# The first stage of a hybrid attention and RWKV block: modulation weights summed in whole rows, x normed in place, one-pass transposes kept in SBUF, and 128 rows in the decay's lower terms

## The chip, the cores and the metric

The kernel runs on one core of one Trainium2 chip. The metric is the device time of one execution in microseconds (us). Before the change it is 1717.37 us, the median of three runs (1715.96 to 1721.29).

## What is computed

The block takes x (1024 tokens by 1024 columns) and a conditioning vector c, everything in float32. The part that matters here is its beginning:

```python
mod = silu(c) @ w_mod + b_mod                  # w_mod is 1024 x 6144
shift1, scale1, gate1, shift2, scale2, gate2 = split(mod, 6)
u = rms_norm(x, ln1_g) * (1 + scale1) + shift1
proj = u @ w_in                                # q k v f | r k v xw xa xg | gates
p = p + (token_shift(p) - p) * mu              # on the RWKV part
w_log = -softplus(-(w0 + tanh(xw) @ w2)) - 0.5
a = sigmoid(a0 + xa @ a2)
g = sigmoid(xg) @ g2
# ... then attention, the RWKV recurrence, their merge, and a convolutional feed-forward layer
```

Only shift1 and scale1 are needed before the first projection. The columns xw and xa (64 each) and xg (128) of the projection are its "low" columns, two tiles of 128 output channels; they come first, since the decay and the gates of the recurrence are made from them.

## The kernel before, in words

All products are made channel by channel: a tile of 128 weight columns is TensorE's stationary operand, and 512 tokens (one "half" of the sequence) are streamed through. For float32 accuracy each operand is split into an upper part (rounded to fp32r) and a lower part (the rest), and a product is the sum of three: upper x upper, lower x upper and upper x lower. So u is held as u_hi and u_lo, eight tiles of 128 channels by 1024 tokens each, and each weight tile as hi and lo. The order of TensorE (PE) is the order of the code in the whole kernel. In the first stage, the prelude, the same holds for VectorE (DVE), ScalarE (ACT) and SyncE (SP, which issues the DMAs); behind it a scheduler orders those.

The prelude goes over 16 blocks: eight channel tiles `kt`, two halves each. Its steps in the code before:

- `load_x` (L408) loads x in eight row tiles, `square` (L415) makes the sums of squares on ACT, and `norm_x` (L419) makes 1/rms (`rstd`) and writes it into diagonal matrices `dg` of 128x128.
- `mod_load` (L426) loads, for one channel tile, the 128 columns of shift1 and of scale1 from all 1024 rows of w_mod, in runs of 128 values (512 bytes). `mod_scale` (L439) sums the scale on PE in eight one-column products; `mod_shift` (L443) sums the shift on DVE in eight steps of 128x128, and `mod_sum` (L453) adds over the partitions on PE. `mod_col` (L456) adds the bias and makes A1 = (1 + scale1) * ln1_g.
- `turn` (L461) multiplies four x tiles by the diagonals, which transposes and norms them in one product; `u_upper` (L467) applies A1 and the shift on ACT and casts to u_hi; `u_lower` (L473) makes u_lo on DVE.
- `low_part` (L477) makes the six products of a block with the two low weight tiles (24 and 25 of w_in). They are summed over the eight channel tiles in four PSUM banks.
- `warm` (L434) issues products without use, which only keep PE busy.
- At the end `low_out` (L490) shifts the sums by one token, and `w2l` (L567, on POOL, the GpSimd engine) is made: the lower part of w2 and a2. Its rows 0 to 63 hold w2's, its rows 64 to 127 a2's. w2 and a2 stand twice one above the other in `w2h`.

Then `shifted` (L346) makes k, r and v of the first head pair (`ps_rkv`: 24 products of 512 columns each, from weight tiles 16, 12 and 20), and between these products `lora` (L603) makes the decay and a, in eight groups of four products `zp`: for each of w2 and a2, w2h with the 128 rows of `xs` (64 rows of its upper part, 64 of its lower), then `w2l` with the 64 rows of the upper part alone (L628). PSUM for `ps_rkv` has two banks, so the third (v) waits for the evacuation of the first (k), which is an instruction of DVE, L358. A ring of two buffers, `raw`, holds every weight tile on its way in (L249, L486), and w2 too.

Of the kernel before, what the change touches and what calls it, by code (L numbers as in the profile page):

```python
# [15 lines left out]
D = 1024  # L16
S = 1024
KT = 8
# [113 lines left out]
def hybrid_block(ctx: ExitStack, tc: tile.TileContext, a, out):  # L132
# [13 lines left out]
    def f32(ap):  # L146
        return ap.bitcast(F32)
# [187 lines left out]
    with ExitStack() as es:  # L335
# [63 lines left out]
        w2l = xp.tile([128, 512], F32R, name="w2l")  # L399
# [3 lines left out]
        with tc.tile_pool(name="st", bufs=1) as st, tc.tile_pool(name="stp", bufs=2, space=PS) as stp, \  # L403
                tc.manual_schedule(engines={mybir.EngineType.SP, mybir.EngineType.DVE, mybir.EngineType.Activation}):
            ssq = st.tile([128, 8], F32, name="ssq")
            rstd = st.tile([128, 8], F32, name="rstd")

            def load_x(half):  # L408
                xs = []
                for t in range(half * 4, half * 4 + 4):  # L410
                    xs.append(st.tile([128, D], F32, tag="xt", name=f"xt{t}", bufs=8))
                    nc.sync.dma_start(xs[-1], a["x"][t * 128 : t * 128 + 128, :])
                return xs

            def square(t):  # L415

                nc.scalar.activation(u_lo[:, 6 + t // 4, :], xs[t], AF.Square, accum_out=ssq[:, t : t + 1])

            def norm_x(half):  # L419

                hs = slice(half * 4, half * 4 + 4)
                rms_rstd(rstd[:, hs], ssq[:, hs])
                for j in range(half * 4, half * 4 + 4):
                    ts(dg[:, j, :], ident, rstd[:, j : j + 1], None, op0=ALU.mult)

            def mod_load(kt):  # L426

                ws = [st.tile([128, D], F32, tag="mw", name=f"wm{i}{kt}", bufs=9) for i in range(2)]
                for i, w in enumerate(ws):
                    nc.sync.dma_start(w.rearrange("p (c n) -> p c n", n=128),  # L430
                                      a["w_mod"].rearrange("(c p) n -> p c n", p=128)[:, :, i * D + kt * 128 : i * D + kt * 128 + 128])
                return ws

            def warm(n):  # L434

                for _ in range(n):
                    mm(idle[:, 0:NC1], cst[:, 0:128], cst, start=True, stop=True)

            def mod_scale(kt, ps):  # L439
                for ci in range(KT):  # L440
                    mm(ps[:, 1:2], mw[kt][1][:, ci * 128 : ci * 128 + 128], sc[:, ci : ci + 1], start=ci == 0, stop=ci == KT - 1)

            def mod_shift(kt):  # L443
                acc = st.tile([128, 128], F32, tag="acc", name=f"acc{kt}", bufs=2)
                for ci in range(KT):
# [1536 lines left out]
```

## Time and profile before

| | |
|---|---|
| time, median of three runs | 1717.37 us (1715.96 to 1721.29) |
| profiled execution, from its first to its last instruction (span) | 1713.2 us; the median of the runs lies 4.2 us above it |
| PE busy in the span | 1665.3 us (97%) |
| DVE, ACT, POOL busy | 1213.0, 813.1, 143.5 us |
| mean granted TensorE clock | 0.986 |
| prelude: first product of `ps_rkv` | 88.04 us after the span's start |
| granted clock, 60 to 70 us | 0.50 |

How to read the profile: a row of the timeline has the start in us, the length in us, the engine, the line of the code, the operation, what it writes and reads, its shape and how many equal ones follow each other; in brackets stands how long the engine sat idle before it and what ended that. PEld is PE's weight load, which overlaps its products. A row of the table by stretches has, for each engine, busy us and the number of instructions, then the clock granted to TensorE (1.00 is full), the DMA engines' share and GB/s.

### The profile page before, as it was taken

The numbers are of one execution on the slowest core, as the hardware profiler recorded it, in microseconds if no ns is written. First come the engines' busy times: TensorE is split into PE (matmuls) and PEld (weight loads), VectorE is DVE, ScalarE is ACT, GpSimd is POOL, SyncE is SP. The second block draws the span as 40 slices with busy tenths as digits, with TensorE's granted clock in tenths as the row PEclk, the third lists the DMA queues.
The fourth block names the chain that finished last, engine by engine and source line by source line (L and its number), as shares of the span: only waits on it lengthen the run. The fifth ranks groups of instructions, "written<-read, shape, count | busy, mean of one in ns | idle before, by whom it ended". The sixth has DMA issues, their size and how long they took to land.

```text
span 1713.2 us, 26506 instructions
## 1 busy us (share of the span) xinstructions
PE 1665.3 (97%) x9984; PEld 1367.0 (80%) x9984; DVE 1213.0 (71%) x2432; ACT 813.1 (47%) x1482; POOL 143.5 (8%) x175
## 2 busy tenths in 40 slices
PE   8899999999999999999999999999999999999998
PEld 7867777787777777888878888888888888888886
DVE  4576687777677632889777734897777777786677
ACT  5364343334344454766652314664444444454455
POOL 0001011111110002323212100000000000000000
PEclk9899999999999999999999999999999999999999
DMA  9287644533333226434268611132333223484463
GB/s 310 89 304 236 185 133 112 140 96 116 95 96 98 85 81 158 135 100 125 75 231 288 255 50 62 57 105 98 106 116 111 93 99 117 149 293 153 123 215 111
DMA packets 135311, 239.87 MB, mean 140 GB/s; under 512 B 39888, under 2 KB 64720, under 8 KB 135184
## 3 DMA queue, kind: packets, MB, share of 16 engines
q1 hardware_dynamic: 127232, 220.94, 39.8%
q0 software_dynamic: 7952, 17.25, 3.7%
q8 instruction: 78, 1.28, 0.3%
q14 instruction: 49, 0.40, 0.1%
HBM read 172.59 MB, written 65.54 MB: 139 GB/s over the span
## 4 chain that ended last, share of the span: by engine, by line
PE 80%; DVE 9%; DMA 4%; ACT 3%; SPq 2%; issue 1%; DVEq 0%; ACTq 0%; POOLq 0%
PE X L140 13%; PE D L140 12%; PE Y L140 6%; PE wo L140 5%; PE gt L140 5%; PE br L140 5%; PE ps_rkv L140 5%; PE qk L140 4%; PE rk_ps L140 4%; PE W L140 3%; PE lg L140 2%; PE ov L140 2%; PE tr L140 2%; PE sp L140 2%; PE tp L144 2%
## 5 line engine op out<-in xcount | busy, mean ns | idle before, releaser
L140 PE MATMUL D<-op,op 128*128 128x512 f32 x924 | 209.8, 389 | 0.0
L140 PEld LDWEIGHTS D<-op,op 128*128 128x128 f32 x924 | 173.3, 188 | 36.3 <-DVE op L1245 0.3
L140 PE MATMUL X<-T_m,S 128*128 128x512 f32 x440 | 107.3, 390 | 0.1
L140 PEld LDWEIGHTS X<-T_m,S 128*128 128x128 f32 x440 | 82.4, 188 | 18.2 <-ACT T_m L1670 0.6
L1244 ACT CAST op<-g 128x512 fp32r<-128x512 f32 x77 | 47.8, 621 | 73.0 <-PE D L140 47.9
L1245 DVE TENSOR_TENSOR op<-g,op 128x512 fp32r<-128x512 f32 x77 | 53.0, 689 | 40.9 <-ACT op L1244 40.8
L1481 DVE SCALAR_TENSOR_TENSOR c<-ab,vec,c 128x512 f32<-128x512 f32 x88 | 65.9, 749 | 19.5 <-ACT c L1484 17.9
L263 DVE TENSOR_TENSOR lo_in<-raw_in,hi_in 128x512 fp32r<-128x512 f32 x84 | 56.4, 706 | 31.6 <-PE gt L140 12.3
L796 DVE TENSOR_TENSOR t<-E,M 128x60 f32<-128x60 f32 (+24 forms) x248 | 56.8, 229 | 29.5 <-DMA M<-sm 24.2
L1445 DVE TENSOR_TENSOR S<-ur,S 128x512 fp32r<-128x512 f32 x66 | 45.5, 691 | 35.6 <-ACT S L1441 35.5
L261 ACT CAST hi_in<-raw_in 128x1024 fp32r<-128x1024 f32 x42 | 43.9, 1047 | 52.5 <-PE ps_rkv L140 17.2
L1441 ACT CAST S<-ur 128x512 fp32r<-128x512 f32 x66 | 41.0, 622 | 55.6 <-DVE ur L1434 30.6
L1445 DVE TENSOR_TENSOR A<-ur,A 128x512 fp32r<-128x512 f32 x64 | 44.0, 688 | 30.9 <-ACT A L1441 30.7
L140 PE MATMUL Y<-T_h,A 128*128 128x512 f32 x264 | 63.5, 389 | 0.0
L140 PE MATMUL Y<-T_h,S 128*128 128x512 f32 x264 | 63.3, 389 | 0.0
L140 PE MATMUL X<-B_b,A 128*128 128x512 f32 x252 | 60.8, 390 | 0.0
L140 PE MATMUL W<-B_f,A 128*128 128x512 f32 x252 | 60.6, 389 | 0.0
L1066 ACT ACTIVATE P<-lg,nm 128x896 f32<-128x896 f32 (+3 forms) x64 | 47.5, 744 | 22.1 <-DVE nm L1062 21.9
L140 PEld LDWEIGHTS Y<-T_h,A 128*128 128x128 f32 x264 | 49.6, 188 | 10.4
L798 DVE TENSOR_TENSOR E<-E,t 128x60 f32<-128x60 f32 (+24 forms) x248 | 53.7, 216 | 5.8
L140 PEld LDWEIGHTS Y<-T_h,S 128*128 128x128 f32 x264 | 49.5, 188 | 10.3
L1441 ACT CAST A<-ur 128x512 fp32r<-128x512 f32 x64 | 39.9, 623 | 34.2 <-PE X L140 31.5
(472 smaller groups left out, 4213.3 us busy)
## 6 DMA issues: line engine op xcount, KB each, us to landing
raw_in<-in_w_in SPq DMA_DIRECT2D x50, 512.0 KB, 3.7
wm<-in_w_mod SPq DMA_DIRECT2D x48, 512.0 KB, 6.5
ur<-in_w_up SPq DMA_DIRECT2D x44, 512.0 KB, 4.0
g<-d_g SPq DMA_DIRECT2D x35, 512.0 KB, 3.9
d_g<-gs SPq DMA_DIRECT2D x44, 256.0 KB, 2.0
d_g<-c SPq DMA_DIRECT2D x33, 256.0 KB, 4.4
d_st<-qh SPq DMA_DIRECT2D x64, 128.0 KB, 2.4
d_gate<-gs SPq DMA_DIRECT2D x32, 256.0 KB, 2.6
```

Source lines behind the costliest of these rows:

```text
L140: nc.tensor.matmul(o, lhsT, rhs, start=start, stop=stop, skip_group_check=more)
L144: nc.tensor.transpose(o, i, eye)
L261: nc.scalar.copy(hi, raw)
L263: nc.vector.tensor_tensor(lo[:, c : c + NH], raw[:, c : c + NH], f32(hi[:, c : c + NH]), op=ALU.subtract)
L796: tt(tv, E32[:, 0:J, s : s + 1].to_broadcast([128, J, W]), M32[:, s : s + 1, s + 1 : 32].to_broadcast([128, J, W]), op=ALU.mult)
L798: tt(E32[:, 0:J, s + 1 : 32], E32[:, 0:J, s + 1 : 32], tv, op=ALU.add)
L1066: nc.scalar.activation(e[:, 0:n], lg[:, 0:n], AF.Exp, bias=nm[:, 0:1], accum_out=nm[:, 1:2])
L1244: nc.scalar.copy(hi, src)
L1245: tt(lo, src, f32(hi), op=ALU.subtract)
L1441: nc.scalar.copy(hi, src)
L1445: tt(lo, src, f32(hi), op=ALU.subtract)
L1481: stt(c, ab[:, x + hf * NH : x + hf * NH + NH], V("conv_w", 22 * x + i), c, op0=ALU.mult, op1=ALU.add)
```

## The change

1. w_mod is loaded in 16 whole pieces (rows ci x 128 to ci x 128 + 127 of one of the two segments, 1024 columns in one run of 4 KB). DVE alone sums them, eight into acc0 (shift) and eight into acc1 (scale), in steps of 128x1024; PE adds over the partitions in eight one-column products per segment. The pieces go through a ring of seven buffers: three of their own (`mw`) and four that held x tiles 0 to 3 (`xa`), so piece 3 is loaded when the first half of x has been transposed. Load m+7 takes the buffer of piece m.
2. x is scaled by rstd in place, on DVE, in steps of 128x1024; `turn` transposes it as it is, with the identity and in one pass, and ACT copies the result to `xn`, which keeps all of it. The transposes thus no longer wait for the modulation.
3. When both sums are there, `u_full` applies A1 and the shift on DVE, in place in `xn`, and ACT casts to u_hi. The 16 blocks follow in one run: first weight tile 24 alone for blocks 0 to 2, tile 25 behind its split from block 3 on.
4. `warm` issues 16 products at the start (before: 34, 10 and 16) and four of 512 columns on w_mod pieces later. The table of the sigmoid is loaded before the blocks.
5. `w2l` is made for all 128 rows, and `lora` multiplies it with all 128 rows of `xs`, which adds the product of the two lower parts.

The core of the diff:

```diff
-        w2l = xp.tile([128, 512], F32R, name="w2l")
+        w2l = xp.tile([128, S], F32R, name="w2l")
...
+            def ring(tag, name, dt=F32):
+                return st.tile([128, D], dt, tag=tag, name=name, bufs=3 if tag == "mw" else 4)
+            def mod_load(seg, ci):
+                w = pieces[seg, ci] = ring("mw" if len(pieces) % 7 < 3 else "xa", f"wm{seg}{ci}")
+                nc.sync.dma_start(w, a["w_mod"][ci * 128 : ci * 128 + 128, seg * D : seg * D + D])
...
+                for t in range(half * 4, half * 4 + 4):
+                    ts(xs[t], xs[t], rstd[:, t : t + 1], None, op0=ALU.mult)
             def turn(kt, half):
                 ps = stp.tile([128, NH], F32, tag="tp", name=f"tr{half}_{kt}")
                 for j in range(4):
-                    mm(ps[:, j * 128 : j * 128 + 128], xs[half * 4 + j][:, kt * 128 : kt * 128 + 128], dg[:, half * 4 + j, :], start=True, stop=True)
+                    transpose(ps[:, j * 128 : j * 128 + 128], xs[half * 4 + j][:, kt * 128 : kt * 128 + 128], ident)
+                nc.scalar.copy(xn[:, kt, half * NH : half * NH + NH], ps)
+            def mod_add(seg, ci, cols=slice(0, D)):
+                w, s_ = pieces[seg, ci][:, cols], sc[:, ci : ci + 1]
+                if ci == 0:
+                    ts(acc[seg][:, cols], w, s_, None, op0=ALU.mult)
+                else:
+                    stt(acc[seg][:, cols], w, s_, acc[seg][:, cols], op0=ALU.mult, op1=ALU.add)
...
+            def u_full(n):
+                kt, _, cs = block(n)
+                ts(xn[:, kt, cs], xn[:, kt, cs], A1[:, kt : kt + 1], m1[:, kt : kt + 1], op0=ALU.mult, op1=ALU.add)
+                nc.scalar.copy(u_hi[:, kt, cs], xn[:, kt, cs])
...
+            for t in range(4):
+                square(t)
+            norm_x(0)
+            for m in range(3):
+                mod_add(*order[m])
+            for kt in range(KT):
+                turn(kt, 0)
+            for m in range(3, 10):
+                mod_load(*order[m])
+            for t in range(4, 8):
+                square(t)
+            for m in (3, 4):
+                add_ahead(m)
+            norm_x(1)
+            for kt in range(KT):
+                turn(kt, 1)
+            nc.scalar.preload_act_table_set("sigmoid_and_others")
+            for m in range(5, 15):
+                add_ahead(m)
+                if m == 7:
+                    shift_ps = mod_sum(0, 0, KT)
+                if m == 9:
+                    mod_col(0, 0, KT, shift_ps)
+                if m > 10:
+                    warm(1, pieces[order[m]])
+            low.append(low_load(25))
+            low_split(0)
+            for x in range(2):
+                mod_add(1, KT - 1, halves_[x])
+            scale_ps = [mod_sum(1, x * 4, 4) for x in range(2)]
+            mod_col(1, 0, 4, scale_ps[0])
+            u_full(0)
+            mod_col(1, 4, 4, scale_ps[1])
+            for n in range(16):
+                if n < 15:
+                    u_full(n + 1)
+                u_lower(n)
+                low_part(0, n)
+                if n == 2:
+                    low_split(1)
+                if n == 3:
+                    for m in range(3):
+                        low_part(1, m)
+                if n > 2:
+                    low_part(1, n)
+            nc.scalar.copy(w2h, w2)
...
-                nc.gpsimd.tensor_tensor(w2l[rs, :], w2[rs, js], f32(w2h[rs, js]), op=ALU.subtract)
+                nc.gpsimd.tensor_tensor(w2l[:, js], w2[:, js], f32(w2h[:, js]), op=ALU.subtract)
...
-                    yield from lora(p, [(j, [(w2h[:, j * 512 : j * 512 + 512], xs2[j]), (w2l[HS[j]], xs2[j][HS[j]])], None, b) for j, b in enumerate(("w0", "a0"))])
+                    yield from lora(p, [(j, [(w2h[:, j * 512 : j * 512 + 512], xs2[j]), (w2l[:, j * 512 : j * 512 + 512], xs2[j])], None, b) for j, b in enumerate(("w0", "a0"))])
```

Behind the prelude PE's order is the same in both, row for row. Three places in the order are spoken of in the prediction. The first is PE at the end of the first channel tile. Before, the sums of the modulation (`mod`), the transposes (`tr0_1`: half 0, tile 1) and the products of a block (`low`) take turns:

```order
L140 MATMUL mod1_312<-cst_73,acc1_321 128x1
L140 MATMUL tr0_1_337<-xwa_124,xt0_140 128x128
L140 MATMUL tr0_1_337<-xwa_124,xt1_142 128x128
L140 MATMUL tr0_1_337<-xwa_124,xt2_144 128x128
L140 MATMUL tr0_1_337<-xwa_124,xt3_146 128x128
L140 MATMUL low01_225<-u_hi_110,hi_in24_154 128x512
L140 MATMUL low11_227<-u_hi_110,hi_in25_158 128x512
```

Now all 64 transposes stand ahead of the first sum, and both sums and the four `idle` products (with pieces 11 to 14 of w_mod, `wm13` to `wm16`) ahead of the first product of a block:

```order
L144 MATMUL tr1_7_314<-cst_73,xt7_163 128x128
L140 MATMUL mod00_334<-cst_73,acc0_139 128x1 x8
L140 MATMUL idle_142<-wm13_263,cst_73 128x512
L140 MATMUL idle_142<-wm14_321,cst_73 128x512
L140 MATMUL idle_142<-wm15_324,cst_73 128x512
L140 MATMUL idle_142<-wm16_331,cst_73 128x512
L140 MATMUL mod10_369<-cst_73,acc1_140 128x1 x4
L140 MATMUL mod14_374<-cst_73,acc1_140 128x1 x4
L140 MATMUL low00_361<-u_hi_110,hi_in24_329 128x512
L140 MATMUL low00_361<-u_hi_110,lo_in24_330 128x512
```

The transposes were between the products of the blocks and are now ahead of them, and a sum for all eight channel tiles stands where a sum for one stood.

The second place is DVE while w_mod is summed. Before, one channel tile's sum took two rows, of 128x128, between two blocks:

```order
L448 TENSOR_SCALAR acc1_321<-wm01_168,sc_90 128x128
L450 SCALAR_TENSOR_TENSOR acc1_321<-wm01_168,sc_90,acc1_321 128x128 x7
L457 TENSOR_TENSOR m1_103<-mod1_312,vec_72 128x2
L459 SCALAR_TENSOR_TENSOR A1_102<-m1_103,vec_72 128x1
L475 TENSOR_TENSOR u_lo_111<-uf1_0_309,u_hi_110 128x512
```

Now it is a run of 128x1024 steps, with one that reads PE's sum of the shift (`mod00`, row L460) among the scale's; the names count segment and piece, so `wm12` is piece 2 of the scale:

```order
L450 SCALAR_TENSOR_TENSOR acc0_139<-wm07_250,sc_90,acc0_139 128x1024
L448 TENSOR_SCALAR acc1_140<-wm10_252,sc_90 128x1024
L450 SCALAR_TENSOR_TENSOR acc1_140<-wm11_254,sc_90,acc1_140 128x1024
L460 TENSOR_TENSOR m1_103<-mod00_334,vec_72 128x8
L450 SCALAR_TENSOR_TENSOR acc1_140<-wm12_260,sc_90,acc1_140 128x1024
```

Row L460 is new in this place: the scale's last six additions stand behind it on DVE, and its own input behind all transposes on PE.

The third place is DVE some way behind the prelude, where k of the first head pair (`k00`) is evacuated. Before:

```order
L221 SCALAR_TENSOR_TENSOR acc2_866<-wm2_1_883,sc_90,acc2_866 128x1024
L648 TENSOR_TENSOR wf_1034<-wr_1035,wf_1034 128x8x8
L358 SCALAR_TENSOR_TENSOR k00_746<-ps_rkv40_766,omu_80,sh_rkv40_791 128x512
L352 MEMSET sh_rkv00_829 128x1
L584 TENSOR_TENSOR xs0_739<-xwa_124,xs0_739 64x1024
```

Now, in the changed kernel's line numbers (13 higher from L567 on):

```order
L221 SCALAR_TENSOR_TENSOR acc2_702<-wm2_1_719,sc_90,acc2_702 128x1024
L661 TENSOR_TENSOR wf_870<-wr_871,wf_870 128x8x8
L597 TENSOR_TENSOR xs0_575<-xwa_124,xs0_575 64x1024
L358 SCALAR_TENSOR_TENSOR k00_582<-ps_rkv40_602,omu_80,sh_rkv40_627 128x512
L352 MEMSET sh_rkv00_665 128x1
```

The lower part of `xs0` (64x1024) has moved from behind the evacuation of k to ahead of it.

177 lines of the change are left out of this document (66 added, 111 removed).

## The prediction

> **What bounds the kernel now.** I read the first part of the page, then the chain of work that ended last, then the table by stretches, then the timeline of the first 130 us.
>
> ```profile
> PE 1665.3 (97%) x9984; PEld 1367.0 (80%) x9984; DVE 1213.0 (71%) x2432; ACT 813.1 (47%) x1482; POOL 143.5 (8%) x175
> ...
> PE 80%; DVE 9%; DMA 4%; ACT 3%; SPq 2%; issue 1%; DVEq 0%; ACTq 0%; POOLq 0%
> ```
>
> PE sets the end: it is busy for 97% of the span, and 80% of the chain is its own. Behind the prelude its order does not change, so what the prelude saves arrives at the end, unless PE then waits for something that was early before. The question is when the first product of `ps_rkv` starts, which I call E. The table by stretches (columns as in the section on the profile) shows where the prelude loses time:
>
> ```profile
> 50.00:60.00 10.00, 5.86 (x34) 5.12 (x34) 4.21 (x11) 3.64 (x5) 0.00 (x0) 0.84 0.44 144
> 60.00:70.00 10.00, 10.00 (x40) 9.14 (x40) 4.28 (x13) 1.40 (x2) 0.00 (x0) 0.50 0.10 37
> ```
>
> PE stands idle for four of the ten us from 50, and in the next ten it is "busy" with 40 products at half clock. The timeline tells why:
>
> ```profile
> 49.23 9.36 SPq L249 DMA_DIRECT2D raw_in<-in_w_in  x2
> ...
> 55.81 1.04 ACT L261 CAST hi_in<-raw_in 128x1024 fp32r<-128x1024 f32 x1 [6.84 <-DMA raw_in<-in_w_in]
> ...
> 60.96 3.41 PE L140 MATMUL mod<-sc,wm 128*128 128x1 f32 x16
> ...
> 88.04 1.99 PE L140 MATMUL ps_rkv<-u_hi,hi_in 128*128 128x512 f32 x8
> ...
> 91.68 1.98 PE L140 MATMUL ps_rkv<-u_hi,lo_in 128*128 128x512 f32 x8
> ```
>
> The cast of a later weight stands in ACT's queue ahead of the next u_hi and waits for its load, ACT 6.84 us with it; PE runs dry and its clock falls. E is 88.04. The sixteen products from there to 91.68 take 3.64 us, 0.228 each at full clock.
>
> **The change, part by part.** First, how fast the pieces of w_mod come:
>
> ```profile
> 14.00:20.00 6.00, 5.96 (x34) 5.87 (x33) 2.74 (x7) 3.36 (x5) 0.00 (x0) 0.72 1.02 404
> 22.00:42.00 20.00, 19.23 (x118) 17.50 (x119) 10.50 (x32) 9.68 (x18) 0.00 (x0) 0.91 1.20 291
> ```
>
> From 14 to 20 us mostly whole rows (x, w_in) were in flight, at 404 GB/s; from 22 to 42 mostly w_mod in runs of 512 bytes, at 291 with busier DMA engines. A piece of 512 KB takes 1.30 us at the one rate and 1.80 at the other; I take 1.30 for whole rows. The Trainium skill (DMA: Bandwidth & Descriptors, Specifications) asks only for 512 bytes per transfer to reach the full rate, so by it the pieces would come no faster than before; the two rows speak against it, and in the sum below 1.80 would move E by 1 us at most, since DVE adds the pieces later than they land.
>
> Now PE's clock. In the first 30 us the trace has a stretch like the new prelude, with transposes and one-column products alone:
>
> ```profile
> 26.57 1.84 PE L140 MATMUL mod<-sc,wm 128*128 128x1 f32 x16
> ```
>
> ```profile
> 28.00:30.00 2.00, 1.35 (x10) 1.26 (x10) 1.42 (x6) 0.20 (x1) 0.00 (x0) 0.87 1.23 294
> 30.00:32.00 2.00, 2.00 (x9) 1.81 (x9) 0.44 (x1) 0.74 (x1) 0.00 (x0) 0.50 1.19 294
> ```
>
> Behind it the clock is at 0.50, though PE's row says busy. The new order puts all 64 transposes and the sums in one such run, so I take half clock from the 16 idle products at the start to the first `low` product, and full clock as the other end. The Trainium skill (TensorE: Matmul & The Clock Gate, Part 4) says that transposes do not count as work for the clock, which is the same choice; were they to count, the second rival below would hold.
>
> The other prices:
>
> ```profile
> 11.36 0.21 ACT L288 ACTIVATE rstd<-rstd 128x4 f32<-128x4 f32 x1
> ...
> 21.11 1.06 ACT L417 ACTIVATE u_lo<-xt 128x1024 fp32r<-128x1024 f32 x1
> ...
> 22.30 1.06 ACT L417 ACTIVATE u_lo<-xt 128x1024 fp32r<-128x1024 f32 x1
> ...
> 85.87 0.62 ACT L471 CAST u_hi<-uf 128x512 fp32r<-128x512 f32 x1
> ...
> 86.52 0.69 DVE L475 TENSOR_TENSOR u_lo<-uf,u_hi 128x512 fp32r<-128x512 f32 x1 [1.60 <-ACT u_hi L471]
> ...
> 93.56 0.75 DVE L219 TENSOR_SCALAR acc<-wm,sc 128x1024 f32<-128x1024 f32 x1
> ...
> 104.47 2.61 DVE L221 SCALAR_TENSOR_TENSOR acc<-wm,sc,acc 128x1024 f32<-128x1024 f32 x2
> ...
> 191.74 0.27 PE L144 MATMUL vt<-cst,v 128*128 128x128 f32 x1
> 191.85 0.27 PE L144 MATMUL at<-cst,ar 128*128 128x128 f32 x1
> ```
>
> ```profile
> L1521 ACT COPY x<-X 128x512 f32<-128x512 f32 x22 | 12.9, 586 | 26.3 <-PE X L140 26.3
> ```
>
> ```profile
> L507 DVE TENSOR_TENSOR lo_in<-raw_in,hi_in 128x1024 fp32r<-128x1024 f32 x2 | 2.4, 1224 | 2.7 <-ACT hi_in L505 2.7
> L1072 DVE TENSOR_SCALAR P<-P,nm 128x512 f32<-128x512 f32 x8 | 3.9, 487 | 0.3
> ```
>
> ```profile
> raw_in<-in_w_in SPq DMA_DIRECT2D x8, 512.0 KB, 4.0
> ```
>
> With these the new prelude runs as follows, the loads of the first four x tiles being unchanged.
>
> - rstd is there at 11.57, and four scalings of 0.75 end at 14.6. A tile's four one-pass transposes take 4 x 0.11 at full clock, 0.88 at half, 0.9 with the handover; ACT's copy (0.59) hides behind that. Eight tiles: 21.8 (22 with the last copy).
> - Tile 7's first transpose, at 20.9, frees the first x buffer for piece 3; it lands 4.0 later, at 25, the others 1.30 apart, and piece 15, the last of 13 transfers behind it, at 41.9. Piece 3 and 4 are added (1.31 each) by 27.6. ACT squares the other x tiles behind its copies, 4 x 1.19 + 0.5, until 27.3. Four scalings: 30.6.
> - Second half of the transposes: 37.9. Behind them on PE stands the sum of the shift, 16 one-column passes, 3.41 at half clock: 41.3. DVE has three additions and two of the scale's done by 36.6 and then stands at row L460, which waits for that sum; the last six additions are queued behind it. This is the new wait of the change: 4.7 us (1.6 if the clock is full).
> - From 41.5: 0.2, five additions 6.5, the split of weight 24 1.22, two half additions of 0.7 each: 50.1 for the first, 50.8.
> - Four sums on PE, 1.7 at half clock: 51.9. Two small steps (0.4), u_full (0.49), the cast (0.62): the first `low` product at 53.5. The second four sums and their steps let DVE finish u_full(1) at 54.5 and u_lower(0) at 55.2.
> - Then a block costs DVE 0.49 + 0.69 = 1.18: u_lower(2) at 57.5. The cast of weight 25 ends on ACT at 58.5, its split on DVE at 59.8, u_lower(3) at 61.0. Block 3's last product of weight 24 waits for that, and 84 products follow it: 84 x 0.228 = 19.2. DVE's own rest is 12 x 1.18 + 1.3 for one weight = 15.5, so PE is last. E is 80.2, against 88.04: **-7.8**. If the clock is full throughout, transposes take 5.6 per half, the sums half, and the same sum gives 74.0: -14.0.
>
> Second, the lower terms of the decay. One of the eight groups:
>
> ```profile
> 107.75 0.39 PE L140 MATMUL zp<-xs,w2h 128*128 128x512 f32 x1
> ...
> 108.07 0.50 PE L140 MATMUL zp<-xs,w2l 64*128 64x512 f32 x1
> ...
> 108.50 0.49 PE L140 MATMUL zp<-xs,w2h 128*128 128x512 f32 x1
> ...
> 108.92 0.49 PE L140 MATMUL zp<-xs,w2l 64*128 64x512 f32 x1
> ...
> 109.34 0.50 PE L140 MATMUL ps_rkv<-u_hi,lo_in 128*128 128x512 f32 x1
> ```
>
> Four products take 1.59; the step from 128 to 64 rows and back costs each of them about 0.2. With 128 rows throughout they are like all others, 4 x 0.228 = 0.91. Eight groups: 8 x 0.68 = **-5.4** on PE, which is the path here. The other end is nothing, if ACT or DVE cannot follow; I take the whole, since PE has no gap there, and DVE and ACT are busy for little more than half of the time:
>
> ```profile
> 110.00:120.00 10.00, 10.00 (x34) 5.48 (x32) 5.19 (x7) 5.89 (x9) 0.49 (x1) 1.00 1.01 386
> ```
>
> Third, what comes late behind E:
>
> ```profile
> 82.50 0.33 SPq L249 DMA_DIRECT2D raw_in<-in_w_in  x1
> ...
> 98.03 0.74 DVE L358 SCALAR_TENSOR_TENSOR k<-ps_rkv,omu,sh_rkv 128x512 f32<-128x512 f32 x1
> ...
> 98.83 1.22 DVE L584 TENSOR_TENSOR xs<-xwa,xs 64x1024 fp32r<-64x1024 f32 x1
> 98.93 2.10 PE L140 MATMUL ps_rkv<-u_hi,hi_in 128*128 128x512 f32 x8
> ```
>
> The 48 products of k and r end about when k is evacuated, and v's first product at 98.93 waits for that evacuation. Now the lower part of `xs0` (1.22) stands ahead of it on DVE, which has no gap there: **+1.2**, between 0 and 1.2. Behind it zp and the next evacuations wait, and they have time. The load of weight 20 waits for w2l, made before when 5.5 us of the prelude were left (82.50). Now w2h is cast after the last u_hi (about 76), w2l by 80, and the load lands at E + 4; SP holds the loads of segment 2 behind it, and DVE's first addition of those, before at E + 5.5, would see at worst 2 us more. I take 0, since they land at E + 5.
>
> At no cost: fewer idle products (before, they filled waits), the sigmoid's table load (ACT waits for the weight there) and w2l's further rows on POOL (the length of a row is the same).
>
> Sum: -7.8 - 5.4 + 1.2 = -12.0 on a span of 1713.2, 1701.2, and with the 4.2 us between span and median 1705.4. I predict 1705.
>
> **The rivals.** *The clock stays full* (transposes count, or the four idle products hold it): -14.0 - 5.4 + 1.2 = -18.2, 1699. For it: in the stretch from 26 to 30 PE also waited, and the new run of transposes is denser. Against it: the row at 30 to 32.
>
> *The lower terms save nothing* (the change does not do what it says there): DVE or ACT sets the pace from E + 14 to E + 37, and 1705.4 + 5.4 = 1711. DVE is then behind with the sums of segment 2; but the profile has no PE idle there now.
>
> *The old wait comes back*: the cast of weight 16 stands on ACT ahead of u_hi(7), and its load is issued only when weight 25 is split, at 59.8. With 4.0 us it lands just as ACT arrives; with 6.6, as at 49.23, PE still has blocks 4 to 6 to do. If it took 10, PE would lose 3.7 us, and if the clock then fell for 13.6 us, as around 60 to 70, half of that as well: about 10 us, 1716, no change.
>
> *Slower*: half clock through all products of the blocks, as before from 60 to 70. 84 x 0.456 = 38.3 instead of 19.2, E at 99.3: +11.3 + 1.2 - 5.4 = +7.1, 1724.5. It turns slower than before when the products take more than 0.371 us each ((88.0 + 4.2 - 61.0)/84). Against it: no one-column products stand between them any more.
>
> **How the numbers follow.** Forecast 0.55, full clock 0.22, nothing from the lower terms 0.13, the old wait 0.06, slower 0.04. A change under 0.3% (5.2 us) cannot be told from none here. The first three are faster, 0.90; I take 0.03 off for several small misses together, which go to no change: faster 0.87, same 0.09, slower 0.04. The range reaches from 1697, a little under the full-clock case, to 1713, a little over the case without the lower terms; it leaves out the old wait in full and the slower case.
>
> **What would show it.** Right: the first `ps_rkv` near 80; DVE's longest wait in the prelude at L460, for PE; a clock of 0.50 between 15 and 50 and 1.00 from 60; zp at 0.23 steps; about 1 us of PE idle ahead of v. Wrong: products of the blocks at half clock; ACT waiting for weight 16's load in the blocks; PE idle among the zp; E under 75 or over 86.

## The result, and the profile after

The changed kernel takes 1702.24 us (median of 4 runs, 1699.63 to 1704.73) against 1718.77 us for the kernel before (4 runs): a ratio of 0.991, 95% interval 0.9892 to 0.9929, so 12 to 19 us faster. The forecast was 1705. The profiled execution is the slowest of the four, 1704.73, with a span of 1703.0; the forecast for the span was 1701.2. The trace of the kernel before, by contrast, has a span of 1713.2, 5.6 us under its median here, so the two traces stand 10.2 us apart where the medians stand 16.5 apart. The total was right, but two of its terms were wrong in opposite directions.

Busy time of the engines and the chain of work, from the page of the changed kernel:

```profile
PE 1638.0 (96%) x9772; PEld 1342.0 (79%) x9772; DVE 1220.8 (72%) x2390; ACT 808.6 (47%) x1482; POOL 143.4 (8%) x175
...
PE 79%; DVE 9%; DMA 6%; ACT 2%; issue 2%; SPq 1%; DVEq 0%; ACTq 0%
```

PE is still the bound, but its busy share fell from 97% to 96%: it stands idle for 65 us of the span instead of 48. The table by stretches of the changed kernel shows the prelude (us, then busy time and count for PE, PEld, DVE, ACT and POOL, then the granted clock, the DMA share and GB/s):

```profile
22.00:42.00 20.00, 12.49 (x56) 7.70 (x56) 16.55 (x17) 10.46 (x18) 0.00 (x0) 0.76 0.96 375
26.00:32.00 6.00, 4.52 (x17) 3.05 (x18) 5.93 (x8) 1.86 (x4) 0.00 (x0) 0.54 1.00 374
32.00:42.00 10.00, 7.97 (x40) 4.65 (x39) 8.25 (x9) 5.16 (x7) 0.00 (x0) 0.99 0.93 371
42.00:52.00 10.00, 6.86 (x23) 5.68 (x24) 7.72 (x15) 2.47 (x5) 0.00 (x0) 0.50 0.47 137
60.00:70.00 10.00, 10.00 (x44) 8.07 (x43) 8.83 (x18) 5.30 (x8) 0.78 (x1) 1.00 0.18 52
```

From 22 to 42 us the loads now come at 375 GB/s; before it was 291. From 60 to 70, where before 40 products ran at half clock, the clock is 1.00. Between 32 and 42 it is full as well, and that was not forecast. The timeline of the prelude, with the rows that answer the forecast:

```profile
23.59 2.61 DVE L450 SCALAR_TENSOR_TENSOR acc<-wm,sc,acc 128x1024 f32<-128x1024 f32 x2 [6.29 <-DMA wm<-in_w_mod]
...
26.11 2.73 DVE L437 TENSOR_SCALAR xt<-xt,rstd 128x1024 f32<-128x1024 f32 x4
...
28.91 5.62 PE L144 MATMUL tr<-cst,xt 128*128 128x128 f32 x29 [0.19 <-DVE xt L437]
34.36 1.84 PE L140 MATMUL mod<-cst,acc 128*128 128x1 f32 x16
36.24 0.17 DVE L460 TENSOR_TENSOR m<-mod,vec 128x8 f32<-128x8 f32 x1 [1.57 <-PE mod L140]
...
43.94 1.41 DVE L450 SCALAR_TENSOR_TENSOR acc<-wm,sc,acc 128x512 f32<-128x512 f32 x2
44.83 3.54 PE L140 MATMUL mod<-cst,acc 128*128 128x1 f32 x16 [2.94 <-DVE acc L450]
48.34 0.80 PE L140 MATMUL low<-u_hi,hi_in 128*128 128x512 f32 x1
55.33 0.71 PE L140 MATMUL low<-u_lo,hi_in 128*128 128x512 f32 x1 [2.14 <-DVE u_lo L481]
57.73 1.04 ACT L261 CAST hi_in<-raw_in 128x1024 fp32r<-128x1024 f32 x1 [0.28 <-DMA raw_in<-in_w_in]
76.73 2.01 PE L140 MATMUL ps_rkv<-u_hi,hi_in 128*128 128x512 f32 x8
```

The shift's sum of 16 passes takes 1.84 us, so the clock had become full within the transposes ahead of it. The same 16 passes for the scale take 3.54 at 44.83: by then PE had stood idle and the clock had fallen. ACT's wait for weight 16 is 0.28 us instead of 6.84. The first `ps_rkv` product, E, comes at 76.73 (the row in the fence stands for eight products), 11.3 us earlier than before and 3.5 earlier than forecast.

Behind E, the rows of PE, ACT, SP and DVE in the changed kernel:

```profile
88.75 2.09 PE L140 MATMUL ps_rkv<-u_hi,hi_in 128*128 128x512 f32 x8 [0.95 <-DVE sh_rkv L352]
91.82 0.39 PE L140 MATMUL zp<-xs,w2h 128*128 128x512 f32 x1
92.05 0.39 PE L140 MATMUL zp<-xs,w2l 128*128 128x512 f32 x1
...
98.60 1.27 ACT L629 ACTIVATE z<-zp,vec 128x512 f32<-128x512 f32 x2 [0.19 <-PE zp L140]
100.02 0.88 SPq L634 DMA_DIRECT2D d_lora<-z  x2
...
110.41 1.26 ACT L629 ACTIVATE z<-zp,vec 128x512 f32<-128x512 f32 x2 [3.36 <-DMA d_lora<-z]
111.15 2.06 PE L140 MATMUL f<-u_hi,wf 128*40 128x512 f32 x8 [2.84 <-ACT z L629]
171.92 1.16 PE L140 MATMUL p<-ar,bk 64*128 64x128 f32 x16 [2.04 <-DVE bk L769]
223.82 0.15 DVE L354 COPY sh_rkv<-pv1k 128x1 f32<-128x1 f32 x1
```

And the rows of the kernel before at the same three places:

```profile
124.96 2.02 PE L140 MATMUL f<-u_hi,wf 128*40 128x512 f32 x8
184.19 1.16 PE L140 MATMUL p<-ar,bk 64*128 64x128 f32 x16 [0.69 <-DVE bk L756]
235.06 0.15 DVE L354 COPY sh_rkv<-pv1k 128x1 f32<-128x1 f32 x1
```

The `zp` products go at 0.23 us as forecast. But PE then waits 2.84 us for ACT, and ACT waits for a store of z to land before it may write z again: the second pair of z tiles is written by 99.87 and its stores are issued from 100.02, but the first of them has landed only at 110.4. The copy in the last row serves as a mark: 235.06 minus its start is a kernel's lead at the mark, and its lead at E, at `f` and at `p` is counted in the same way from the rows of the kernel before. In the changed kernel the lead is 11.3 us at E, 13.8 at `f`, 12.3 at `p` and 11.2 at the mark: as much as at E, as if the lower terms had brought nothing. That was the question for the experiments.

### The profile page after: what moved, and what is told of

It is laid out like the page before. It is cut to its first block, busy times and chain, and to the rows that moved or that the text cites. A ratio compares the mean times of both kernels' runs of the same rounds, so it can differ in the third digit from the quotient of the medians.

```text
span 1703.0 us, 26042 instructions
## 1 busy us (share of the span) xinstructions
PE 1638.0 (96%) x9772; PEld 1342.0 (79%) x9772; DVE 1220.8 (72%) x2390; ACT 808.6 (47%) x1482; POOL 143.4 (8%) x175
## 4 chain that ended last, share of the span: by engine, by line
PE 79%; DVE 9%; DMA 6%; ACT 2%; issue 2%; SPq 1%; DVEq 0%; ACTq 0%
PE X L140 13%; PE D L140 12%; PE Y L140 6%; PE wo L140 5%; PE br L140 5%; PE gt L140 5%; PE rk_ps L140 4%; PE qk L140 4%; PE ps_rkv L140 4%; PE W L140 3%; PE lg L140 2%; PE v L140 2%; PE ov L140 2%; PE sp L140 2%; PE tp L144 2%
## 5 line engine op out<-in xcount | busy, mean ns | idle before, releaser
L1454 ACT CAST S<-ur 128x512 fp32r<-128x512 f32 x66 | 41.0, 622 | 55.6 <-DVE ur L1447 30.6
L1079 ACT ACTIVATE P<-lg,nm 128x896 f32<-128x896 f32 (+3 forms) x64 | 47.4, 743 | 22.8 <-DVE nm L1075 22.6
```

Source lines behind the costliest of these rows:

```text
L1079: nc.scalar.activation(e[:, 0:n], lg[:, 0:n], AF.Exp, bias=nm[:, 0:1], accum_out=nm[:, 1:2])
L1454: nc.scalar.copy(hi, src)
```

## The experiments

All runs beside one another. E, and the time from E to the first `f` product, are from the profiled execution; median and ratio are from the timed runs, each against runs of the kernel before on the same chip.

| run | E | E to `f` | lead at the mark | median us | ratio (95% interval) |
|---|---|---|---|---|---|
| before | 88.04 | 36.92 | 0 | | 1 |
| after | 76.73 | 34.42 | 11.2 | 1702.24 | 0.991 (0.9892 to 0.9929) |
| prelude_only | 74.98 | 38.05 | 11.1 | 1705.35 | 0.9935 (0.9914 to 0.9956) |
| lower_only | 87.61 | 30.25 | 6.5 | 1711.57 | 0.9969 (0.9953 to 0.9985) |
| before_no_stall | 81.46 | 37.67 | 6.2 | 1711.68 | 0.9968 (0.9955 to 0.9981) |
| runs_512 | 82.03 | 32.32 | 9.0 | 1707.01 | 0.9945 (0.9928 to 0.9961) |
| split_early | 74.84 | 32.69 | 14.7 | 1699.12 | 0.9896 (0.9878 to 0.9914) |
| warm | 90.33 | 32.85 | 1.5 | 1716.98 | 0.9999 (0.9985 to 1.0013) |
| warm_split | 88.17 | 33.01 | 3.4 | 1712.82 | 0.9976 (0.9963 to 0.9989) |
| warm_split_2 | 72.92 | 33.33 | 19.0 | 1697.30 | 0.9891 (0.9877 to 0.9905) |
| seg5_loads_out | 76.88 | 31.39 | 15.4 | 1699.11 | 0.9899 (0.9879 to 0.992) |
| seg5_late | 76.03 | 31.40 | 1.0 | 1715.67 | 0.999 (0.9974 to 1.0006) |
| half_stores | 77.08 | 31.41 | 15.8 | 1700.35 | 0.9907 (0.9894 to 0.992) |
| together | 71.72 | 32.55 | 20.8 | 1696.01 | 0.988 (0.9862 to 0.9899) |

The same prelude (after, prelude_only, seg5_loads_out, seg5_late, half_stores) gives E between 74.98 and 77.08, so a difference of 2 us in E is not yet a finding. By the timed runs alone, only lower_only, before_no_stall, warm, warm_split and seg5_late can be told from the changed kernel; the intervals of all others overlap its own, and what is said of them below rests on one trace each.

### The two parts apart

**prelude_only**: the changed kernel with the lower terms as they were.

```diff
-        w2l = xp.tile([128, S], F32R, name="w2l")
+        w2l = xp.tile([128, 512], F32R, name="w2l")
...
-  ... (w2l[:, j * 512 : j * 512 + 512], xs2[j]) ...
+  ... (w2l[HS[j]], xs2[j][HS[j]]) ...
```

> The changed kernel with the lower terms of the decay back at 64 rows; the prelude stays new. Theory A (behind the first ps_rkv product PE's lead over the kernel before is cut back to what the loads and the chain to bk allow, so that the 5.4 us of the lower terms are spent again by 210 us): the first ps_rkv product at 76.7, the zp products as before, PE never waits for ACT's z, and at 210 to 230 us the lead is 10 to 11.3 us, against 11.15 in the changed kernel; median 1702 to 1704. Theory B (the lower terms pay, and it is the lead from the prelude that is given back): lead 11.15 - 5.4 = 5.8 us, median about 1707.5.

**lower_only**: the same lines the other way round, in the kernel before.

> The kernel before with the lower terms of the decay at 128 rows; the old prelude. Theory A: the zp products go at 0.23 us, PE is about 5 us ahead of the kernel before at the end of the zp groups, then waits for ACT's z (a store of z not landed) and for bk, and at 210 to 230 us has a lead of 0 to 1.5 us; median 1717 to 1719, no change that can be told. Theory B: the 5.4 us stay, median 1713.3.

First prelude_only, then lower_only, at `f` and at the mark:

```profile
113.03 2.02 PE L140 MATMUL f<-u_hi,wf 128*40 128x512 f32 x8
223.94 0.15 DVE L354 COPY sh_rkv<-pv1k 128x1 f32<-128x1 f32 x1
```

```profile
117.86 2.01 PE L140 MATMUL f<-u_hi,wf 128*40 128x512 f32 x8
228.58 0.16 DVE L354 COPY sh_rkv<-pv1k 128x1 f32<-128x1 f32 x1
```

prelude_only reaches the mark as early as the whole change does, as theory A has it; its median, 1705.35, lies between the two theories. But lower_only does not give its gain back: it is 7.1 us ahead at `f`, 0.4 of that from E, and still 6.5 at the mark, where theory A expected 1.5 at most. That is theory B's figure, so the lower terms pay when they stand alone. Nothing fixed in time stands behind E, and theory A falls in that form. By the timed runs the parts add up: 11.2 us (7.6 to 14.8) and 5.3 us (2.6 to 8.1) make 16.5, and the whole change measures 15.5 (12.2 to 18.6). In the profiled executions the loss needs both: neither part alone makes PE wait for z. In lower_only the DMA engines are as full (1.02 from 108 to 118 us), and ACT waits there 1.6 us in all for stores of z, which does not reach PE; in the changed kernel it waits 5.4. SP's order of these stores and loads differs between the two, and the runs do not separate that from the time at which they fall. Nor do full engines alone decide it: in prelude_only their share is 0.98 to 0.99 from 96 to 116 us, and a store of z lands after 6.3 us (median) instead of the 8.6 of the changed kernel.

### What PE waits for behind the lower terms

**seg5_loads_out**: seven loads of 512 KB fewer while the z tiles are stored; the additions all use the first piece, so the sums of segment 5 are not those of the reference.

```diff
-            w = pool.tile(shape, F32, tag=tags[1], name=f"wm{seg}_{kt}", bufs=3)[:, 0:D]
-            nc.sync.dma_start(w, a["w_mod"][kt * 128 : kt * 128 + 128, seg * D : seg * D + D])
+            if seg != 5 or kt == 0:
+                w = pool.tile(shape, F32, tag=tags[1], name=f"wm{seg}_{kt}", bufs=3)[:, 0:D]
+                nc.sync.dma_start(w, a["w_mod"][kt * 128 : kt * 128 + 128, seg * D : seg * D + D])
```

> The changed kernel, with seven of the eight loads of segment 5 of w_mod left out (all eight additions use the first piece, so the values that segment 5 gives are not the reference's): 3.7 MB less in the stretch from 86 to 120 us, where the DMA engines are full. Theory A1 (the store of z lands late because the DMA engines are full): PE's wait of 2.84 us for z at 111 shrinks under 1 us and the lead at 140 to 160 grows from 13.7 to about 16. Then, if the chain to bk is set by DVE, ACT and the stores of the q and k tiles, PE's wait for bk grows from 2.0 to 4 or more and the lead at 190 stays near 12, median 1702. Rival A2 (the z wait is ACT's own lateness): the z wait stays at 2 to 3 us. Rival A3 (nothing catches up): lead 14 to 15 at 210 to 230, median 1699.

The stretch from 100 to 120 us in the changed kernel, and in seg5_loads_out, by the table of stretches:

```profile
100.00:120.00 20.00, 17.16 (x76) 12.75 (x75) 13.31 (x14) 11.33 (x16) 4.68 (x3) 1.00 0.99 372
```

```profile
100.00:120.00 20.00, 20.00 (x90) 14.38 (x89) 18.68 (x19) 12.23 (x17) 5.04 (x3) 1.00 0.66 244
```

With the DMA engines busy for 0.66 of the time instead of 0.99, PE has no gap. A store of z lands after 5.5 us (median) instead of 8.6. PE's wait for z is gone, its wait for `bk` falls from 2.04 to 1.45, and the lead at the mark is 15.4. A1 holds, and so does A3: what is saved there is not taken by the chain to `bk`. A2 falls.

**half_stores**: no load less, but each half of z stored as soon as it is written.

```diff
+                    for z, (i, _, _, _) in zip(zs, parts):
+                        nc.sync.dma_start(d_lora[i, p][:, cs], z[:, cs])
                     yield 1000
-                for z, (i, _, _, _) in zip(zs, parts):
-                    nc.sync.dma_start(d_lora[i, p], z)
```

> The changed kernel with each z tile of the lower terms stored in two halves, each as soon as it is written, instead of whole. Theory A1 (z's ring is held up by stores that land late): the first half of a store is out some 4 us earlier and the second is half as long, so PE's wait for z of 2.84 us goes under 1.0, the lead at 140 grows from 13.7 to 15 or more, and at 210 to 230 to 12.5 or more. Rival A5 (the engines are full, so a store lands when the loads ahead of it are through, however it is cut): the wait stays at 2 to 3 us, lead 11 to 12.

```profile
108.49 2.01 PE L140 MATMUL f<-u_hi,wf 128*40 128x512 f32 x8
219.26 0.15 DVE L354 COPY sh_rkv<-pv1k 128x1 f32<-128x1 f32 x1
```

No wait at `f`, and a lead of 15.8 at the mark with E unchanged, though the DMA engines are as full as in the changed kernel (a share of 1.04 from 100 to 120 us): A1 holds, and A5 falls. In the timed runs this is 0.9907 against 0.991, which the intervals do not tell apart. So the wait is certain for the profiled execution of the changed kernel; whether its faster executions have it too is not known, since only one of them has a trace.

**seg5_late**: the same loads, put in order behind the stores.

```diff
+            if seg == 5 and kt < 3:
+                tc.add_manual_dep(i.ins, marks["z"].ins.name, NOSYNC)
...
+                    marks["z"] = nc.sync.dma_start(d_lora[i, p], z)
```

> The changed kernel with the loads of segment 5 of w_mod ordered behind the stores of the eight z tiles on SP; no work is left out. Theory A1 (the z stores land late because the DMA engines are full with those loads): PE's wait of 2.84 us for z goes under 0.5, the lead at 140 us grows from 13.7 to 16 or more, and at 210 to 230 from 11.2 to 14 to 15.5; median 1698 to 1700. Rival A4 (the additions of segment 5, now later, hold up DVE and with it the chain to bk or the second sum): a new wait of 2 us or more between 130 and 180 and no gain at 230.

```profile
154.99 3.78 PE L140 MATMUL mpb<-acc,cst 128*128 128x512 f32 x4 [12.82 <-DVE acc L223]
```

The wait for z went, and the lead grew until there. But rival A4 came true, and at six times the size I gave it: six of the eight additions of segment 5 came among and behind the third group of z tiles, from 140.33 to 153.65, and some of them waited there for their loads, up to 3.35 us. PE stood 12.82 us for their sum. Cutting the stores is the better remedy, since it makes nothing late.

### What the prelude's gain is made of

**before_no_stall**: the kernel before with the cast of weight 16 ordered behind the last u_hi on ACT.

```diff
-            nc.scalar.copy(hi, raw)
+            i = nc.scalar.copy(hi, raw)
+            if "u" in marks and name == "in16":
+                tc.add_manual_dep(i.ins, marks.pop("u").ins.name, NOSYNC)
...
```

> The kernel before, with the cast of weight 16 moved in ACT's queue behind the last u_hi; nothing else. Theory D (most of what the new prelude gains is the old wait for that weight and the clock that fell with it): PE runs through from 50 to 70 at full clock, 4 us of idle time and half of 13.6 us are gone, and one to two us come back since the first ps_rkv product waits for that cast and split: first product at 78 to 80 against 88.04, median 1708 to 1711. Rival D2 (the additions of 128-column pieces or the loads at 291 GB/s hold PE anyway): 84 or later, median 1714 to 1718.

```profile
81.46 1.99 PE L140 MATMUL ps_rkv<-u_hi,hi_in 128*128 128x512 f32 x8
```

The row answers to 88.04. Theory D is right in kind, and 1.5 us too large: 6.6 of the 11.3 us of the new prelude are the old stall and the clock that fell with it, and one dependency removes them; PE does not wait from 50 to 70 us any more, and the clock is 1.00 there. The other 4.7, give or take the 2 us by which E scatters, come from the new order.

**runs_512**: the changed kernel, with pieces made of every other block of 128 columns.

```diff
-nc.sync.dma_start(w, a["w_mod"][ci * 128 : ci * 128 + 128, seg * D : seg * D + D])
+nc.sync.dma_start(w.rearrange("p (c n) -> p c n", n=128),
+                  a["w_mod"][ci * 128 : ci * 128 + 128, 0 : 2 * D].rearrange("p (c s n) -> p c s n", s=2, n=128)[:, :, seg, :])
...
```

> The changed kernel with the same pieces of w_mod, in the same number of transfers and the same order, but each piece made of every other 128-column block of both segments, so that a transfer consists of runs of 512 bytes as in the kernel before; the blocks of the sums are renamed to match, and all results are the same. Theory F (short runs come at the 291 GB/s that the kernel before shows, 1.80 us a piece instead of 1.30): the pieces come later than DVE adds them, the last at about 47, the last half addition ends at 48.4 instead of 45.35, and the first ps_rkv product is at 79 to 80 instead of 76.7; median 1704 to 1706. The prediction's bound was 1 us at most (77.7). Rival F2 (the rate of the kernel before was low for another reason, and runs of 512 bytes cost nothing): 76 to 77, median 1702. This is what the Trainium skill (DMA: Bandwidth & Descriptors, Specifications) would give, which asks for 512 bytes per transfer for the full rate.

Its table of stretches, its additions on DVE and its E:

```profile
22.00:42.00 20.00, 11.05 (x52) 7.33 (x52) 14.89 (x16) 10.35 (x19) 0.00 (x0) 0.71 1.20 294
```

```profile
43.76 1.28 DVE L451 SCALAR_TENSOR_TENSOR acc<-wm,sc,acc 128x1024 f32<-128x1024 f32 x1 [1.61 <-DMA wm<-in_w_mod]
46.90 1.28 DVE L451 SCALAR_TENSOR_TENSOR acc<-wm,sc,acc 128x1024 f32<-128x1024 f32 x1 [1.86 <-DMA wm<-in_w_mod]
...
49.24 1.41 DVE L451 SCALAR_TENSOR_TENSOR acc<-wm,sc,acc 128x512 f32<-128x512 f32 x2
```

```profile
82.03 2.01 PE L140 MATMUL ps_rkv<-u_hi,hi_in 128*128 128x512 f32 x8
```

The same bytes come at 294 GB/s instead of 375, DVE waits for late pieces, the last half addition starts its pair at 49.24 instead of 43.94, and E moves by the same 5.3 us. Theory F holds, with its size short by 2 us, and F2 falls. The Trainium skill (DMA: Bandwidth & Descriptors, Specifications) gives 512 bytes per transfer as enough for the full rate. This run does not bear that out: 294 GB/s stand against 375 with rows of 4 KB. With short runs the new prelude would be no faster than the old one without its stall (81.46).

### What is left in it

**split_early**: weight 25 split while DVE stands for the scale's sum, its products block by block.

```diff
+            low_split(1)
             mod_col(1, 0, 4, scale_ps[0])
...
                 low_part(0, n)
-                if n == 2:
-                    low_split(1)
...
-                if n > 2:
-                    low_part(1, n)
+                low_part(1, n)
```

> The changed kernel with the split of weight 25 ahead of the first block, in the time that DVE stands waiting for the scale's sum, and its products block by block. PE's wait of 2.1 us at 55.3 goes: 8 products at half clock from 48.3, then 88 at 0.228, so the first ps_rkv product at 72 instead of 76.7. Theory A (the loads behind it move with the prelude's end, so an earlier end is kept in part): lead at 210 to 230 us 13 to 16, median 1698 to 1700. Theory B (loads and the chain to bk stand where they were in time): the lead stays at 11 to 12 and the median at 1702.

```profile
49.26 0.79 PE L140 MATMUL low<-u_hi,hi_in 128*128 128x512 f32 x1
...
54.80 0.63 PE L140 MATMUL low<-u_lo,hi_in 128*128 128x512 f32 x1
55.23 0.49 PE L140 MATMUL low<-u_hi,hi_in 128*128 128x512 f32 x1
```

E moved by 1.9 us instead of 4.7, to 74.84, which is no more than E scatters. The wait went, but the first twelve products ran at half clock, 0.43 us apart where none had to wait, until 55.2. The lead at the mark rose from 11.2 to 14.7, as theory A has it; 1.9 of that is E, and most of the rest is a shorter wait for z at `f`, 1.14 us instead of 2.84.

**warm** and **warm_split**: more idle products, without and with that split.

```diff
             for kt in range(KT):
                 turn(kt, 0)
+            warm(24)
...
-                if m > 10:
-                    warm(1, pieces[order[m]])
+                if m > 7:
+                    warm(3, pieces[order[m]])
...
+            warm(6, f32(low[0][1]))
```

> The changed kernel with more idle products on PE in the prelude: 24 behind the first half's transposes, three in place of one behind each of the last additions, six behind the split of weight 24. They have no result. Theory C (what is left in the prelude is the clock): the granted clock is full from 27 to 60 us, the sums of the scale take 1.84 us instead of 3.54, no block product takes 0.43, and the first ps_rkv product comes at 73.8 instead of 76.7. Rival C2 (DVE's chain of additions and the split of weight 25 set the end whatever the clock is): 76 to 77. Rival C3 (the idle products run at half clock themselves and delay the transposes): 78 or later.

> The idle products of the run warm together with the early split of weight 25. split_early alone moved the first ps_rkv product by 2.1 us only, with its block products at half clock until 55.4. Theory C: with a full clock the 96 products follow one another from 47.5, 21.9 us, so the first ps_rkv product is at 69.5 to 70.5, the lead at 210 to 230 us 19 or more, the median 1694 to 1697. Rival C4 (DVE's pace of 1.24 us a block and the split of weight 16 set the end): 71 to 73.

```profile
35.63 18.27 PE L140 MATMUL idle<-wm,cst 128*128 128x512 f32 x42
53.74 5.31 PE L140 MATMUL idle<-hi_in,cst 128*128 128x512 f32 x12
```

Both are failures of my arithmetic: 21 calls are 42 instructions, 0.43 us each even at full clock, and they held up the scale's sum by 14 us. C3 came true, though not for the reason I gave. They say little on theory C: in warm the scale's sum took 1.84 us, at full clock, but the idle products set E.

**warm_split_2**: the split, with 32, one and three calls in those places instead of 24, three and six.

> As warm_split, with idle products that fit into the waits: 32 behind the first half's transposes, one call behind each of the last seven additions (two instructions of 0.43 us at full clock, under the 1.31 of an addition) and three behind the split of weight 24; in warm_split 42 and 12 of them took 18.3 and 5.3 us and delayed the sums of the scale by 14 us. Theory C: full clock through the block products, which follow one another from 47.5: first ps_rkv product at 69.5 to 71, lead at 210 to 230 us 17 to 19, median 1694 to 1697. Rival C4 (DVE's pace sets the end): 72 to 74, as in split_early. Rival C3 (they hold up the transposes or the sums): 76 or later.

```profile
45.98 1.92 PE L140 MATMUL mod<-cst,acc 128*128 128x1 f32 x16
49.19 0.79 PE L140 MATMUL low<-u_hi,hi_in 128*128 128x512 f32 x1 [1.29 <-ACT u_hi L477]
```

The sum of the scale now takes 1.92 us instead of 3.54, as theory C has it, but the first block products still fell into a stretch of half clock (0.79 in the mean from 47 to 55 us), and E is 72.92. That is in C4's range, but not by C4's mechanism: from the first block product to E, PE waits for nothing. A first product 1.7 us later than forecast and the half clock are what theory C missed.

**together**: warm_split_2 and half_stores, and the shift's column step four additions later.

```diff
-                if m == 9:
+                if m == 13:
                     mod_col(0, 0, KT, shift_ps)
```

> The edits of warm_split_2 and half_stores together, and the shift's column step (which reads the sum of the shift, DVE's row L460) moved four additions back, so that DVE no longer stands there for PE. Theory G (that wait, 1.57 us in the changed kernel and 2.2 in warm_split_2, lies on the path, as the prediction put it): the first ps_rkv product is 1.5 to 2.2 us earlier than the 72.7 of warm_split_2, at 70.5 to 71.2; with no wait for z the lead at 210 to 230 us is 21.5 to 23; median 1693.5 to 1696. Rival G2 (the pieces of w_mod come no earlier, so DVE waits for them instead): first product at 72 to 73, lead 20 to 21, median 1695.5 to 1697.5.

The column step and the first block product in together:

```profile
39.73 0.16 DVE L460 TENSOR_TENSOR m<-mod,vec 128x8 f32<-128x8 f32 x1
...
40.45 1.28 DVE L450 SCALAR_TENSOR_TENSOR acc<-wm,sc,acc 128x1024 f32<-128x1024 f32 x1 [0.55 <-DMA wm<-in_w_mod]
...
47.30 0.50 PE L140 MATMUL low<-u_hi,hi_in 128*128 128x512 f32 x1 [0.79 <-ACT u_hi L477]
...
53.94 0.50 PE L140 MATMUL low<-u_hi,hi_in 128*128 128x512 f32 x1 [0.54 <-ACT u_hi L477]
...
55.35 0.50 PE L140 MATMUL low<-u_lo,hi_in 128*128 128x512 f32 x1 [0.68 <-DVE u_lo L481]
```

DVE no longer waits at L460, though 0.55 us of that come back as a wait for a piece of w_mod; the first block product comes 1.9 us earlier than in warm_split_2, and the block products run at full clock. But PE now waits 0.54 us for u_hi and 0.68 for u_lo among the blocks, and E is 71.72, 1.2 earlier: between G (70.5 to 71.2) and G2 (72 to 73), and within the scatter of E. The lead at the mark, 20.8, and the median are those that G2 gave. So the wait at L460 held up the first block product, as G has it, but that E gains by its removal is not shown. PE still waits 0.9 us for z. At 0.988 (0.9862 to 0.9899) this is the lowest ratio of all; the changed kernel's 0.991 (0.9892 to 0.9929) overlaps its interval.

## Why the prediction was right, point by point

- **The scalings, the first transposes, piece 3** (14.6, 21.8, 25 forecast): 14.0, 20.4, 23.59. Right, and 0.6 to 1.4 us early.
- **Half clock until the first `low` product.** This step failed, on the safe side. The second half's transposes ran at half clock at first and at full clock from about 32, and they ended at 34.5 instead of 37.9. About half of those 3.4 us is that the scalings ended at 28.84 and not at 30.6. The rest is the clock, and three transposes that went in between the scalings: behind these the transposes took 5.6 us instead of 7.3. The Trainium skill (TensorE: Matmul & The Clock Gate, Part 4) says that transposes do not count as work for the clock. The trace speaks against it: the granted clock is 0.54 in the stretch from 26 to 32, in which PE has transposes alone, and 0.99 behind it. The row that I had taken as evidence (30 to 32 us in the kernel before) came behind a stretch of one-column passes and a wait, from 26.57 to 29.06, and the `tr` products of that kernel are ordinary products with a diagonal. Were transposes to count, I wrote, the second rival would hold; I meant the first in the list, the full clock, and it held for part of the way.
- **DVE stands at L460 for 4.7 us**: 1.57, the value that I gave for a full clock. It was not the longest wait either: DVE waited 6.29 us for piece 3.
- **The scale's sum at half clock, the first `low` product at 53.5**: half clock, yes (3.54 for 16 passes), but at 48.34, since all ahead of it was early.
- **Block 3 waits for the split of weight 25; 84 products of 0.228 follow**: the wait is there (2.14 us at 55.33), and the products took 21.4 us instead of 19.2, since the clock fell once more behind that wait. (The sum also left out the product that waits, 0.2 us.) E: 76.73 against 80.2 forecast and 74.0 for the rival of a full clock. It lies between the two, since the clock did.
- **Pieces at 1.80 us would move E by 1 us at most.** This bound failed: runs_512 moved it by 5.3. I had assumed that DVE adds later than the pieces land; at the lower rate it is the other way round.
- **The lower terms, -5.4**: mis-sized. The time from E to `f` fell by 6.7 us in lower_only. The product behind each group is quicker too, 0.23 us to the next instead of 0.34, which my four products did not count; that is 0.9 us of the 1.3. The rest stays open: E to `f` differs by 0.75 us between before and before_no_stall as well, which do the same work there.
- **k's evacuation, +1.2**: 0.95.
- **Nothing else comes late behind E.** This step failed. I asked whether loads would be late for DVE, and not what the faster groups ask of the stores: ACT may not write a z tile before the store of the pair two earlier has landed, and with full DMA engines that took 10 us. PE lost 2.84 us there, 1.35 more at `p` and 1.0 more up to the mark. The rival that took the lower terms for nothing named the right place and the wrong engine, and "PE idle among the zp", which I had listed as a sign against the forecast, did appear at their end.

So -12.0 on the span stands against -10.2 in the profiled execution: E brought 3.5 more than forecast and the lower terms 0.9 more (36.92 - 34.42, and the waits of 0.95 and 2.84), 5.2 were lost between the `zp` products and the mark, and 1.0 behind it; about 0.2 is not accounted for. That the sum came out so near is luck: a loss that I had put at nothing ate up a gain that I had not counted. In the median of the timed runs, where the gain is 15.5, less seems to be lost; no trace shows those executions.

## What to carry to other kernels

When a stage becomes faster, look at what it hands on as well as at what it takes: here a ring of buffers that are emptied by stores held up its writer while the DMA engines were full, and storing each half as soon as it was done took the wait away. Before rebuilding a stage, undo its longest wait by itself: here one dependency brought 6.6 of the 11.3 us. And price idle products from a row of the same shape before using them as cover.

## What the runs showed of the hardware

- The granted clock is full or half, and its stretches are multiples of about 3.41 us. In the changed kernel it is half from 21.3 to 31.6 us, full to 41.8, half to 52.0, full to 55.4, half to 58.9 and then full. As far as these steps show, each followed what PE had done in the one before: 3.12 us of transposes (28.14 to 31.55) made the next full, a step of almost nothing but one-column passes (45.20 to 48.60) left it at half, and a step with 1.27 us of work (52.03 to 55.44) was followed by half clock. Where the steps fall against the work differs from one execution to the next. In prelude_only, with the same prelude, PE's wait for weight 25 was spread over two steps, each with over 2.6 us of work, and the clock stayed full behind it; E is 74.98, against 76.03 to 77.08 in the four others.
- Behind the mark all kernels do the same work, and the time from the mark to the end went with the sum of the half-clock stretches in it: 1476.0 us in together with 22.8 us of half clock, 1478.2 in the kernel before with 28.3, 1484.3 in before_no_stall with 42.1. Over all fourteen traces that is about 0.44 us for each us at half clock. In the largest set of timed executions of one kernel, 35 of the kernel before, the mean granted clock accounts for 0.7 of the variance of the span.
- Runs of 512 bytes came at 294 GB/s with a DMA share of 1.20, and whole rows of 4 KB at 375 with a share of 0.96.
- Products of 64 rows that alternate with products of 128 took longer than products of 128 rows throughout: four of them 1.59 us instead of 0.91, and eight such groups 6.7 us more from E to `f`.
